# A two-layer decoder trunk on one core: residual tiles kept on chip, heads' outputs 0 to 3 stored unsplit

## The chip, the core and the metric

The kernel runs on one core of a Trainium2 chip. The metric is the device time of one execution in microseconds (us). TensorE (PE) multiplies matrices; VectorE (DVE), ScalarE (ACT) and GpSimd (POOL) work on tiles of 128 partitions; SyncE (SP) and POOL issue the DMAs between DRAM and the chip's memory. Each engine has its own queue of instructions and works it off in order; an instruction that waits for another engine or for a DMA holds up all behind it on its engine.

## The reference

One sequence of 1024 tokens, width 1024, float32, two layers, and a final normalisation.

```
h = x
n = rms_norm(h, attn_norm[0])
h = h + hybrid_mixer(n)         # layer 0: 8 heads of dilated attention, 8 of forgetting
h = h + conv_glu_ffn(rms_norm(h, ffn_norm[0]))
n = rms_norm(h, attn_norm[1])
h = h + diff_mixer(n)           # layer 1: 8 heads of differential attention
h = h + conv_glu_ffn(rms_norm(h, ffn_norm[1]))
out = rms_norm(h, final_norm)

forgetting_attention: softmax(q k^T + c_t - c_s) v, causal; c = cumsum(log_sigmoid(n w_f + b_f))
differential_attention: (softmax(q1 k1^T) - lam softmax(q2 k2^T)) v, rms_norm of each head's output
both mixers end in: concat(heads) @ w_out
conv_glu_ffn: (silu(conv3(n w_gate)) * (n w_up)) @ w_down, inner width 2816
```

## The kernel before

All tiles hold features on the 128 partitions and tokens on the free axis, so a layer's residual h is 8 feature blocks (index m) of 2 token halves (half 0 and 1) of 512 tokens: 16 tiles of 128x512. A float32 product is made of three matmuls: each operand is split into a high part (a rounded copy, made by ACT) and a low part (source minus high part, by DVE), and hi·hi, hi·lo, lo·hi are added up in PSUM. This `split` (L162) is the commonest step of the kernel.

Time runs as follows: attention of layer 0 (start to about 612 us), its feed-forward `channel(0)` (to about 1300), attention of layer 1 (about 1360 to 1862), `channel(1)` (to the end). In the attention phases `weave` (L489) merges two streams by a planned goal of work done: the *units* (one head or pair of heads and one token half: scores D, exponentials e, transposes T split into ph and pl, and the output O) and the *jobs* (projections for later heads, then the output projection, one generator step at a time). A job can carry `after`, the unit that must have ended before it starts. The compiled order of each engine's queue is fixed; the tile framework puts the instructions in it and the waits between them.

The places that matter here:

- `out_heads` (L291) takes a finished head output (o2 in layer 0, Ra in layer 1; index k from 0 to 7 in each layer). For k of 6 and 7 it is split into tiles that stay on chip (oh__, ol__). For k of 0 to 5 it is split into so_h and so_l, and both are stored to DRAM (od), 256 KB each.
- `job_load` (L429) fetches both parts again: for k of 0 to 3 behind the last projection job, so 16 loads of 256 KB in a row; for 4 and 5 later. They go through POOL's queue (`store` is a DMA on POOL, `put` one on SP).
- `job_out` (L441) is the output projection, in three jobs: heads 0 to 3 for both halves, added to the residual rt and stored to hp; heads 4 to 7 for half 0, added to the reloaded hp tile and stored again, with the sums for the norm; heads 4 to 6 for half 1 (`rest`), stored again. The last head's part of half 1 is done in `channel` (L1360), with weights o7.
- Between the second and the third job, `stats` makes the norm's rows for half 0, and `blocks` (L1174) reloads the eight hp tiles of half 0 on SP, scales each (`token_blocks`, L1118), stores it to nt, and splits it into nh and nl for the gate product. This is one generator step: all eight follow each other at once.
- `channel` (L1323) reloads the eight half-1 tiles of hp into x (tag wq, 16 slots), adds the last head's product, makes the norm, scales, and forms sums and differences with the half-0 tiles b0 (reloaded from nt: four in wq slots, four in bt slots), which are split again (`cut`, tiles bt) as operands of the feed-forward. The feed-forward's weights use the other wq slots, and POOL makes sums of weights there (L824).
- The pool `big` has 32 tiles of 128x512; nh, nl, oh__, ol__, rt and the token tiles share it.

Of the kernel before, what the change touches and what calls it, by code (L numbers as in the profile page):

```python
# [49 lines left out]
class Trunk:  # L50
# [240 lines left out]
    def out_heads(self, o, half, k):  # L291

        if k not in self.odirect:
            self.split_out(o, half, None, self.od[0][k], self.od[1][k], 0)
            return
        self.O[k, half] = (self.big.tile([P, HT], F32R, name="oh_", tag="big"),
                           self.big.tile([P, HT], F32R, name="ol_", tag="big"))
        self.split(*self.O[k, half], o)
# [37 lines left out]

    def job_rope(self, s1, s2, n, scale, dst, r):

        w1, w2 = self.wadd8(s1), self.wadd8(s2)

        def gen():
            for half in range(2):
                x1 = self.pj()
                yield from self.g_mm(x1, w1, n, half)
                ab = self.rope_a(x1, half)
                x2 = self.pj()
                yield from self.g_mm(x2, w2, n, half)
                self.rope_b(ab, x2, half, scale, dst, r)
        return Job(gen, 4 * 8 * 0.64)

    def job_plain(self, src, n, scale, dst, r):
        nc = self.nc
        w = self.wadd8(src)

        def gen():
            for half in range(2):
# [4 lines left out]
                nc.vector.tensor_tensor(o, x, n["rb"][:, c], ALU.mult)  # L361
                self.split_out(o, half, scale, dst[0], dst[1], r)
        return Job(gen, 2 * 8 * 0.64)

# [64 lines left out]
    def job_load(self, O, k, after):  # L429
# [9 lines left out]
        return Job(gen, 0.0, after)  # L439

    def job_out(self, w, ks, halves, O, base, evict, after, depth=5):  # L441

# [46 lines left out]
    def weave(self, ev, jobs, deadline, margin):  # L489
# [24 lines left out]
        st = {"job": 0, "gen": None, "done": 0.0}  # L514
        fins = set()
        lastq = max(k for k, e in enumerate(ev) if e[1] == 1)
# [607 lines left out]
    def run(self):  # L1124
# [22 lines left out]
        Os = [{}, {}]  # L1147
        self.odirect = (6, 7)
        cs = [slice(hf * HT, (hf + 1) * HT) for hf in range(2)]


        def out_jobs(l, w, base):
            st, gi, O = stF[l], 2 * l + 1, Os[l]

            def add(src, norm):
                def b(m, half):
# [17 lines left out]
            def blocks():  # L1174
                ts = []
                for m in range(10):
                    if m < 8:
                        t = f(self.big.tile([P, HT], F32R, name="t0", tag="big"))
                        self.put(t, parts[l][m][:, cs[0]])
                        ts.append(t)  # L1180
                    if m == 0:
                        rest.fetch()
                    if 0 < m < 9:
                        self.token_blocks(st, gi, 0, m - 1, ts[m - 1])
                        self.store(half0[m - 1], ts[m - 1])
                    if m > 1:
                        hl = (self.big.tile([P, HT], F32R, name=x, tag="big") for x in ("nh", "nl"))
                        st["h"][m - 2, 0], st["l"][m - 2, 0] = hl
                        self.split(st["h"][m - 2, 0], st["l"][m - 2, 0], ts[m - 2])
                yield 0.0  # L1190
# [3 lines left out]
            jobs += [self.job_out(w, [0, 1, 2, 3], [0, 1], O, *add(base, False), last(3))]  # L1194
            jobs += [self.job_load(O, k, last(k)) for k in range(4, 6)]
            jobs += [self.job_out(w, [4, 5, 6, 7], [0], O, *add(part, True), 29 if l == 0 else 13)]
            rest = self.job_out(w, [4, 5, 6], [1], O, *add(part, False), 27 if l == 0 else 14, 3)
            jobs += [Job(stats, 1.3), Job(blocks, 0.0)]
            jobs += [rest]
            return jobs  # L1200
# [14 lines left out]
        for g in range(2):  # L1215
# [3 lines left out]
            for p in range(2 * g, 2 * g + 2):  # L1219
                J0 += [self.job_plain(w[2 * p], n, -0.125, qB, p * P),  # L1220
                       self.job_plain(w[2 * p + 1], n, None, kB, p * P)]
        J0 += out_jobs(0, a["woA"], lambda m: a["xT"][m * P:(m + 1) * P, :])
# [5 lines left out]
        for g in range(4):  # L1228
            w = a["wqkC"]
            if g:  # L1230
                J1 += [self.job_v(a["wvC"][g], n, 2, P, (1, 2 * g))]
            J1 += [self.job_rope(w[4 * g], w[4 * g + 1], n, -0.125, qC, g * P),
                   self.job_rope(w[4 * g + 2], w[4 * g + 3], n, None, kC, g * P)]
        J1 += out_jobs(1, a["woC"], lambda m: hs[m])
# [88 lines left out]
        def channel(l, es, w7, F, after, mid):  # L1323
# [310 lines left out]
```

## Time and profile before

| | us |
|---|---|
| median of three runs | 2571.03 (2567.0 to 2571.26) |
| the profiled execution | 2565.89, its span 2564.1 |
| PE busy | 2467.2 (96%), 12511 matmuls |
| DVE busy | 1979.0 (77%) |
| ACT busy | 1221.5 (48%) |
| POOL busy | 721.4 (28%) |
| moved by DMA | 536.96 MB, mean 209 GB/s |

The span runs from the first to the last recorded instruction; the execution is 1.8 us longer. PE's clock has two levels, 1.2 and 2.4 GHz; a granted clock (PEclk) of 1.00 means the higher one all through a stretch. A row of waits says which engine and line waited for which other engine, line and tile. In names like oh__6277 the number tells tiles of one name apart. "<-" reads "is written from".

### The profile page before, as it was taken

What the parts mean: (1) busy time and instruction counts of PE and PEld (TensorE: products, weight loads), DVE (VectorE), ACT (ScalarE), POOL (GpSimd) and SP (SyncE); (2) the same over time, 40 slices, a digit from 0 to 9 for tenths busy, and PEclk for the clock granted to TensorE, in tenths of its full rate; (3) what the DMA queues carried; (4) which work ended last, traced back from release to release, by engine and by line L of the source; (5) the groups of instructions that cost most, each with busy time, mean ns of one, the idle gap of its engine ahead of it and who ended that gap; (6) DMA issues with size and microseconds to landing.
All of it is one profiled execution on the core that took longest, in us unless ns stands there. A gap on an engine that the chain in (4) does not pass through costs nothing.

```text
span 2564.1 us, 38450 instructions
## 1 busy us (share of the span) xinstructions
PE 2467.2 (96%) x12511; PEld 2047.6 (80%) x12511; DVE 1979.0 (77%) x3885; ACT 1221.5 (48%) x2443; POOL 721.4 (28%) x978
## 2 busy tenths in 40 slices
PE   8999999998899999999999999989888999999998
PEld 7899898776688888778888888877666888887886
DVE  7778878776988988775666888878769878977656
ACT  5456655454544344454434555545454443435433
POOL 1211112222444665100021211232225456740000
PEclk9999999998999999999999999999989999999998
DMA  5655556867766887664555555696576677766644
GB/s 192 229 172 172 178 173 216 255 204 275 216 207 219 244 241 240 205 220 167 193 202 169 197 182 193 203 288 216 179 253 198 204 238 242 248 201 231 226 130 160
DMA packets 249240, 536.96 MB, mean 209 GB/s; under 512 B 37976, under 2 KB 50896, under 8 KB 249040
## 3 DMA queue, kind: packets, MB, share of 16 engines
q1 hardware_dynamic: 179792, 320.02, 39.3%
q0 software_dynamic: 68672, 213.96, 25.1%
q8 instruction: 99, 1.62, 0.3%
q14 instruction: 101, 0.83, 0.1%
q10 hardware_dynamic: 576, 0.52, 0.1%
HBM read 362.33 MB, written 172.03 MB: 208 GB/s over the span
## 4 chain that ended last, share of the span: by engine, by line
PE 79%; DVE 8%; DMA 7%; ACT 3%; issue 2%; SPq 0%; POOL 0%; DVEq 0%; ACTq 0%; POOLq 0%
PE pj L145 67%; PE D L145 5%; PE O L145 4%; PE T L148 3%; DVE wl L131 2%; DMA wr<-in_wgate 1%; DVE bt L166 1%; PE small L145 1%; DMA wr<-in_wdown 1%; ACT wh L129 1%; DVE e L590 1%; DMA ncb<-cd 1%; ACT e L739 1%; DMA wr<-in_wqkC 1%; DMA ar<-td 1%
## 5 line engine op out<-in xcount | busy, mean ns | idle before, releaser
L145 PE MATMUL pj<-bt,wh 128*128 128x512 f32 x1760 | 554.2, 395 | 13.0 <-DVE bt L166 8.6
L145 PEld LDWEIGHTS pj<-bt,wh 128*128 128x128 f32 x1760 | 331.2, 188 | 93.5 <-DVE bt L166 11.6
L131 DVE TENSOR_TENSOR wl<-wr,wh 128x512 fp32r<-128x512 f32 (+2 forms) x340 | 235.7, 696 | 180.8 <-ACT wh L129 171.1
L145 PE MATMUL pj<-nh,wh 128*128 128x512 f32 x864 | 356.9, 413 | 16.8 <-ACT nh L232 8.6
L129 ACT ACTIVATE wh<-wr 128x512 fp32r<-128x512 f32 (+2 forms) x340 | 211.4, 624 | 290.5 <-PE pj L145 122.5
L145 PE MATMUL pj<-bt,wl 128*128 128x512 f32 x880 | 347.7, 395 | 0.0
L145 PE MATMUL pj<-nl,wh 128*128 128x512 f32 x864 | 346.2, 401 | 0.0
L145 PE MATMUL pj<-nh,wl 128*128 128x512 f32 x864 | 346.0, 401 | 0.0
L131 DVE TENSOR_TENSOR wl<-wq,wh 128x512 fp32r<-128x512 f32 x268 | 278.0, 1038 | 30.4 <-ACT wh L129 30.2
L129 ACT ACTIVATE wh<-wq 128x512 fp32r<-128x512 f32 x268 | 166.7, 628 | 239.2 <-PE pj L145 186.9
L824 POOL TENSOR_TENSOR wq<-wq 128x512 f32<-128x512 f32 x132 | 195.3, 1491 | 211.4 <-DVE wl L131 102.3
L145 PE MATMUL pj<-ah,wh 128*128 128x512 f32 (+1 forms) x628 | 248.0, 396 | 2.5 <-ACT s L1086 1.2
L145 PE MATMUL pj<-ah,wl 128*128 128x512 f32 (+1 forms) x628 | 246.2, 393 | 0.0
L145 PE MATMUL pj<-al,wh 128*128 128x512 f32 (+1 forms) x628 | 246.1, 392 | 0.0
L145 PEld LDWEIGHTS pj<-nh,wh 128*128 128x128 f32 x864 | 166.1, 192 | 49.9 <-ACT nh L232 8.6
L165 ACT ACTIVATE ph<-T 128x512 fp32r<-128x512 f32 (+3 forms) x288 | 138.9, 486 | 131.5 <-PE T L148 128.7
L145 PEld LDWEIGHTS pj<-bt,wl 128*128 128x128 f32 x880 | 165.8, 188 | 39.0
L145 PEld LDWEIGHTS pj<-nh,wl 128*128 128x128 f32 x864 | 165.5, 192 | 37.9 <-DVE wl L131 0.4
L145 PEld LDWEIGHTS pj<-nl,wh 128*128 128x128 f32 x864 | 166.2, 192 | 31.1 <-DVE nl L247 0.5
L166 DVE TENSOR_TENSOR pl<-T,ph 128x512 fp32r<-128x512 f32 (+3 forms) x288 | 157.5, 552 | 34.2 <-ACT ph L165 32.9
L148 PE MATMUL T<-ident,e 128*128 128x128 f32 x864 | 144.1, 277 | 19.2 <-DVE e L746 13.5
L145 PE MATMUL pj<-wh,nh 128*128 128x256 f32 (+1 forms) x512 | 149.0, 293 | 0.0
(476 smaller groups left out, 5339.7 us busy)
## 6 DMA issues: line engine op xcount, KB each, us to landing
wq<-in_wgate SPq DMA_DIRECT2D x88, 256.0 KB, 3.7
wq<-in_wup SPq DMA_DIRECT2D x88, 256.0 KB, 3.9
act<-v POOLq DMA_DIRECT2D x44, 512.0 KB, 3.6
td<-sc POOLq DMA_DIRECT2D x80, 256.0 KB, 4.5
wq<-in_wdown SPq DMA_DIRECT2D x80, 256.0 KB, 4.4
sd<-wq POOLq DMA_DIRECT2D x80, 256.0 KB, 4.1
ar<-td SPq DMA_DIRECT2D x80, 256.0 KB, 3.8
wr<-sd SPq DMA_DIRECT2D x80, 256.0 KB, 3.8
```

The lines of the kernel that those rows point to most:

```text
L129: nc.scalar.activation(hi[:, :n], raw[:, :n], AF.Copy)
L131: nc.vector.tensor_tensor(lo[:, :n], raw[:, :n], f(hi[:, :n]), ALU.subtract)
L145: self.last = self.nc.tensor.matmul(*args, **kw)
L148: self.last = self.nc.tensor.transpose(*args)
L165: nc.scalar.activation(hi, src, AF.Copy)
L166: nc.vector.tensor_tensor(lo, src, f(hi), ALU.subtract)
L590: self.nc.vector.tensor_tensor_reduce(out=e[:, k0:k0 + w], in0=d[:, :w], in1=in1(k0, w), scale=1.0, scalar=init, op0=ALU.add, op1=ALU.min, ...
L739: nc.scalar.activation(e[m][:, :W], e[m][:, :W], AF.Exp, scale=-1.0, bias=nm[:, m:m + 1], accum_out=ls[:, m, i4:i4 + 1])
L824: nc.gpsimd.tensor_tensor(dst, x, y, op)
```

## The change

- Heads' outputs 0 to 3 go to DRAM as they are, one store of 256 KB for each half, without a split. `fetch_raw` loads them again, one load for each half, called within the last q/k projection job of the layer when its first half is done. The new first job behind the projections, `job_split`, splits the eight loaded tiles on chip (oh__ from ol__, then ol__ in place).
- The half-0 tiles of the residual stay on chip between the second job and `blocks` (dict t0); the reload is gone. The half-1 tiles stay on chip between `rest` and `channel` (dict t1); their store to hp behind `rest` and the reload are gone. b0 takes eight wq slots.
- `blocks` yields three times behind each token tile, and each yield takes one step of `rest` if the unit that `rest` needs has ended.

```diff
     def out_heads(self, o, half, k):
+        if k in self.oraw:
+            self.store(self.od[0][k][:, half * HT:(half + 1) * HT], o)
+            return
         if k not in self.odirect:
...
     def job_plain(self, src, n, scale, dst, r, between=None):
...
                 self.split_out(o, half, scale, dst[0], dst[1], r)
+                if half == 0 and between is not None:
+                    between()
...
+    def fetch_raw(self, O, after):
+        assert after in self.fins, (after, self.fins)
+        for k in self.oraw:
+            for half in range(2):
+                O[k, half] = (self.big.tile([P, HT], F32R, name="oh_", tag="big"),
+                              self.big.tile([P, HT], F32R, name="ol_", tag="big"))
+                self.store(f(O[k, half][1]), self.od[0][k][:, half * HT:(half + 1) * HT])
+
+    def job_split(self, O):
+        def gen():
+            for k in self.oraw:
+                for half in range(2):
+                    self.split(*O[k, half], f(O[k, half][1]))
+                yield 0.0
+        return Job(gen, 0.0)
...
                 def e(m, half, ps, t):
                     nc.vector.tensor_tensor(t, t, ps, ALU.add)
-                    self.store(parts[l][m][:, cs[half]], t)
-                    if norm:
-                        self.norm_chunk(st, m, half, t, None)
+                    if half == 0 or keep is None:
+                        self.store(parts[l][m][:, cs[half]], t)
+                    if keep is not None:
+                        keep[m] = t
+                        if half == 0:
+                            self.norm_chunk(st, m, half, t, None)
...
             def blocks():
...
+                rest.fetch()
+                more = rest.gen()
+                for m in range(9):
                     if m < 8:
-                        t = f(self.big.tile([P, HT], F32R, name="t0", tag="big"))
-                        self.put(t, parts[l][m][:, cs[0]])
...
+                        self.token_blocks(st, gi, 0, m, t0[m])
+                        self.store(half0[m], t0[m])
...
+                        self.split(st["h"][m - 1, 0], st["l"][m - 1, 0], t0[m - 1])
+                    for _ in range(3):
+                        yield next(more, 0.0) if rest.after in self.fins else 0.1
+                while rest.after not in self.fins:
+                    yield 0.1
+                yield from more
...
-            jobs = [self.job_load(O, k, last(k)) for k in range(4)]
+            jobs = [self.job_split(O)]
...
-            x = [wq() for _ in range(8)]
-            for m in range(8):
-                self.put(x[m], parts[l][m][:, cs[1]])
+            x = [self.t1[l][m] for m in range(8)]
...
-            b0 = [wq() for _ in range(4)] + [f(small()) for _ in range(4)]
+            b0 = [wq() for _ in range(8)]
```

The change moves instructions at three places that the prediction speaks of.

ACT in layer 0, where the loads of heads 0 to 3 land (about 436 us in the trace before; ph is the high part of a transposed tile T, e an exponential, so_h the high part of a projection's result). Before:

```order
L165 ACTIVATE ph_6000<-T_5995 128x4x128
L165 ACTIVATE ph_6020<-T_6016 128x3x128
L165 ACTIVATE ph_6000<-T_6042 128x4x128
L681 ACTIVATE e_6032,st_6033<-e_6032,st_6033 128x256
L165 ACTIVATE ph_6020<-T_6052 128x4x128
L681 ACTIVATE e_6062,st_6063<-e_6062,st_6063 128x384
L165 ACTIVATE ph_6086<-T_6084 128x128
```

and now:

```order
L165 ACTIVATE ph_5960<-T_5955 128x4x128
L165 ACTIVATE oh__6043<-ol__6044 128x512
L165 ACTIVATE oh__6046<-ol__6047 128x512
L165 ACTIVATE oh__6049<-ol__6050 128x512
L165 ACTIVATE ph_5980<-T_5976 128x3x128
L165 ACTIVATE ph_5960<-T_6002 128x4x128
L706 ACTIVATE e_5992,st_5993<-e_5992,st_5993 128x256
L165 ACTIVATE oh__6052<-ol__6053 128x512
L165 ACTIVATE ph_5980<-T_6012 128x4x128
L165 ACTIVATE oh__6055<-ol__6056 128x512
L165 ACTIVATE oh__6058<-ol__6059 128x512
L165 ACTIVATE oh__6061<-ol__6062 128x512
```

The splits oh__ of the loaded tiles ol__ stand among the attention's copies and exponentials.

DVE in layer 0 at the token tiles (about 579 us in the trace before; t0_ and, now, rt_7191, rt_7193, rt_7195 are token tiles, gn and rb the norm's factors, nl the low part, pl the low part of a transposed tile). Before:

```order
L1120 SCALAR_TENSOR_TENSOR t0_7532<-t0_7532,gn_69,rb_7503 128x512
L1120 SCALAR_TENSOR_TENSOR t0_7540<-t0_7540,gn_69,rb_7503 128x512
L1120 SCALAR_TENSOR_TENSOR t0_7544<-t0_7544,gn_69,rb_7503 128x512
L166 TENSOR_TENSOR nl_7549<-t0_7532,nh_7548 128x512
L166 TENSOR_TENSOR pl_7476<-T_7637,ph_7475 128x4x128
L166 TENSOR_TENSOR nl_7557<-t0_7540,nh_7556 128x512
L166 TENSOR_TENSOR pl_7529<-T_7661,ph_7528 128x4x128
L166 TENSOR_TENSOR nl_7565<-t0_7544,nh_7564 128x512
L1120 SCALAR_TENSOR_TENSOR t0_7552<-t0_7552,gn_69,rb_7503 128x512
L1162 TENSOR_TENSOR rt_7536<-rt_7536,pj_7648 128x512
```

and now:

```order
L1145 SCALAR_TENSOR_TENSOR rt_7191<-rt_7191,gn_69,rb_7471 128x512
L1145 SCALAR_TENSOR_TENSOR rt_7193<-rt_7193,gn_69,rb_7471 128x512
L166 TENSOR_TENSOR pl_7444<-T_7543,ph_7443 128x4x128
L166 TENSOR_TENSOR nl_7553<-rt_7191,nh_7552 128x512
L166 TENSOR_TENSOR pl_7497<-T_7572,ph_7496 128x4x128
L1145 SCALAR_TENSOR_TENSOR rt_7195<-rt_7195,gn_69,rb_7471 128x512
L166 TENSOR_TENSOR nl_7585<-rt_7193,nh_7584 128x512
L1189 TENSOR_TENSOR rt_7502<-rt_7502,pj_7559 128x512
L131 TENSOR_TENSOR wl_7596<-wr_7592,wh_7594 128x384
L615 ISA e_7604,mn_7609<-D_7606,ncb_6837 128x512
```

The scalings of three tiles in a row and their subtractions are drawn apart; scores (ISA rows) and the next product's add stand between them.

PE at the end of layer 0's attention (about 611 us; O is the last unit's output, nh and nl times wh and wl the gate product, oh__7929 or oh__7873 times o7_ the last head's part of the output projection). Before:

```order
L145 MATMUL O_7867<-ph_7880,V_6867 128x128
L145 MATMUL O_7867<-pl_7881,V_6867 64x128
L145 MATMUL pj_7955<-nl_7573,wh_7742 128x512
L145 MATMUL pj_7955<-nh_7572,wl_7744 128x512
L145 MATMUL pj_7977<-nh_7548,wh_7803 128x512
L145 MATMUL pj_7977<-nl_7549,wh_7803 128x512
...
L145 MATMUL pj_7977<-nl_7573,wh_7803 128x512
L145 MATMUL pj_7977<-nh_7572,wl_7805 128x512
L145 MATMUL pj_8015<-oh__7929,o7_7939 128x512
L145 MATMUL pj_8015<-ol__7930,o7_7939 128x512
```

and now:

```order
L145 MATMUL O_7808<-pl_7822,V_6835 64x256
L145 MATMUL O_7808<-ph_7821,V_6835 128x128
L145 MATMUL O_7808<-pl_7822,V_6835 64x128
L145 MATMUL pj_7943<-oh__7873,o7_7883 128x512
L145 MATMUL pj_7943<-ol__7874,o7_7883 128x512
L145 MATMUL pj_7951<-oh__7873,o7_7883 128x512
L145 MATMUL pj_7951<-ol__7874,o7_7883 128x512
```

The last head's products follow directly on the last row of O; the gate products that stood between are ahead of it.

## Rows read from the trace of the kernel before

**Rows 1.** Page, busy us, share of the span, instructions of each engine
```profile
PE 2467.2 (96%) x12511; PEld 2047.6 (80%) x12511; DVE 1979.0 (77%) x3885; ACT 1221.5 (48%) x2443; POOL 721.4 (28%) x978
```

**Rows 2.** Stretches: length; busy of PE, PEld, DVE, ACT, POOL; PEclk, DMA share, GB/s
```profile
480.00:520.00 40.00, 40.00 (x226) 33.68 (x225) 27.99 (x64) 14.88 (x32) 8.63 (x16) 1.00 0.70 221
440.00:480.00 40.00, 35.68 (x193) 28.99 (x192) 29.03 (x78) 20.17 (x46) 13.41 (x25) 0.91 0.89 286
560.00:600.00 40.00, 34.38 (x157) 27.43 (x156) 32.24 (x69) 17.75 (x35) 11.33 (x21) 0.83 0.63 213
600.00:640.00 40.00, 35.17 (x163) 27.84 (x162) 22.76 (x43) 17.65 (x32) 8.63 (x16) 0.91 0.78 282
680.00:720.00 40.00, 34.74 (x139) 26.69 (x138) 36.37 (x43) 18.50 (x32) 23.43 (x23) 0.91 0.65 196
1680.00:1720.00 40.00, 33.84 (x171) 28.06 (x170) 29.14 (x69) 18.10 (x42) 13.14 (x25) 0.91 0.95 293
1800.00:1840.00 40.00, 30.15 (x155) 24.52 (x156) 33.89 (x89) 22.29 (x52) 7.02 (x13) 0.87 0.43 156
1840.00:1880.00 40.00, 31.54 (x144) 24.27 (x143) 19.75 (x40) 13.10 (x31) 7.01 (x13) 0.96 0.55 181
1880.00:1920.00 40.00, 34.83 (x134) 27.42 (x135) 29.68 (x51) 20.89 (x36) 12.18 (x19) 0.87 0.83 298
1920.00:1960.00 40.00, 35.28 (x141) 27.51 (x140) 39.75 (x45) 19.79 (x37) 22.79 (x20) 0.91 0.66 202
```

**Rows 3.** Chain that ended last, 425 to 460: start, us, what
```profile
434.25 17.20 DMA ncb<-cd
```

**Rows 4.** DMA issues 425 to 470: count, KB each, us to landing; one in time order
```profile
oh__6277<-od POOLq DMA_DIRECT2D x1, 256.0 KB, 4.7
...
ol__6282<-od POOLq DMA_DIRECT2D x1, 256.0 KB, 8.7
...
oh__6301<-od POOLq DMA_DIRECT2D x1, 256.0 KB, 12.8
...
432.08 0.54 POOL L197 DMA_DIRECT2D ol__6282<-od  x1
```

**Rows 5.** ACT in order of time, 428 to 446: start, us, instruction, idle before
```profile
438.33 0.49 ACT L165 ACTIVATE ph<-T 128x384 fp32r<-128x384 f32 x1 [1.37 <-PE T L148]
```

**Rows 6.** Waits of SP's queue, 540 to 575: us in total, times, longest
```profile
SPq L194 <- DMA hp<-rt: 7.7, 3, 3.4
```

**Rows 7.** DVE and POOL in order of time, three places
```profile
579.21 2.08 DVE L1120 SCALAR_TENSOR_TENSOR t<-t,gn,rb 128x512 f32<-128x512 f32 x3 [1.51 <-ACT rb L282]
...
676.95 5.33 DVE L166 TENSOR_TENSOR bt<-wq,bt 128x512 fp32r<-128x512 f32 x1
...
677.58 4.14 POOL L824 TENSOR_TENSOR wq<-wq 128x512 f32<-128x512 f32 x3
```

**Rows 8.** Waits of PE, 540 to 700
```profile
PE pj L145 <- DVE bt L166: 5.3, 4, 3.8
...
PE D L145 <- DVE mn L590: 2.1, 1, 2.1
PE pj L145 <- DVE wq L1364: 2.0, 2, 1.5
```

**Rows 9.** PE in order of time, 610 to 632
```profile
611.59 0.22 PE L145 MATMUL O<-pl,V 128*64 128x128 f32 x1
...
614.96 0.39 PE L145 MATMUL pj<-oh__7929,o 128*128 128x512 f32 x1
```

**Rows 10.** Waits of DVE, 1670 to 1700
```profile
DVE Ra L795 <- DMA rt<-sr: 6.4, 1, 6.4
```

**Rows 11.** Waits of PE, 1795 to 1990
```profile
PE T L148 <- DVE e L746: 4.5, 1, 4.5
```

**Rows 12.** Tile Ra, 1440 to 1470: durations in ns, first and last start
```profile
L795 DVE SCALAR_TENSOR_TENSOR Ra<-Ra,subg,rt x1: 748/748/748, 1448.1 to 1448.1; 128x512 f32<-128x512 f32 x1
...
L759 ACT ACTIVATE Ra<-O x1: 597/597/597, 1461.6 to 1461.6; 128x512 f32<-128x512 f32 x1
```

More of the change, by code (lines that the diff above doesn't have):

```diff
@@ L335, in pj, with job_rope @@
         return self.psp.tile([P, HT], F32, name="pj", tag=tag)
-    def job_rope(self, s1, s2, n, scale, dst, r):
+    def job_rope(self, s1, s2, n, scale, dst, r, between=None):
         w1, w2 = self.wadd8(s1), self.wadd8(s2)
@@ L348, in gen, with job_plain @@
                 self.rope_b(ab, x2, half, scale, dst, r)
+                if half == 0 and between is not None:
+                    between()
         return Job(gen, 4 * 8 * 0.64)
-    def job_plain(self, src, n, scale, dst, r):
+    def job_plain(self, src, n, scale, dst, r, between=None):
         nc = self.nc
@@ L362, in gen @@
                 self.split_out(o, half, scale, dst[0], dst[1], r)
+                if half == 0 and between is not None:
+                    between()
         return Job(gen, 2 * 8 * 0.64)
@@ L514, in weave @@
         st = {"job": 0, "gen": None, "done": 0.0}
-        fins = set()
+        fins = self.fins = set()
         lastq = max(k for k, e in enumerate(ev) if e[1] == 1)
@@ L1147, in run, with add @@
         Os = [{}, {}]
-        self.odirect = (6, 7)
+        self.odirect, self.oraw = (6, 7), (0, 1, 2, 3)
         cs = [slice(hf * HT, (hf + 1) * HT) for hf in range(2)]
+        self.t1 = {}
         def out_jobs(l, w, base):
             st, gi, O = stF[l], 2 * l + 1, Os[l]
-            def add(src, norm):
+            def add(src, keep=None):
                 def b(m, half):
@@ L1174, in blocks @@
             def blocks():
-                ts = []
-                for m in range(10):
+                rest.fetch()
+                more = rest.gen()
+                for m in range(9):
                     if m < 8:
-                        t = f(self.big.tile([P, HT], F32R, name="t0", tag="big"))
-                        self.put(t, parts[l][m][:, cs[0]])
[L1180 to L1186, printed above, removed]
-                        hl = (self.big.tile([P, HT], F32R, name=x, tag="big") for x in ("nh", "nl"))
-                        st["h"][m - 2, 0], st["l"][m - 2, 0] = hl
-                        self.split(st["h"][m - 2, 0], st["l"][m - 2, 0], ts[m - 2])
@@ L1190, in blocks @@
-                yield 0.0
+                        self.token_blocks(st, gi, 0, m, t0[m])
+                        self.store(half0[m], t0[m])
+                    if m > 0:
+                        hl = (self.big.tile([P, HT], F32R, name=x, tag="big") for x in ("nh", "nl"))
+                        st["h"][m - 1, 0], st["l"][m - 1, 0] = hl
+                        self.split(st["h"][m - 1, 0], st["l"][m - 1, 0], t0[m - 1])
+                    for _ in range(3):
+                        yield next(more, 0.0) if rest.after in self.fins else 0.1
@@ L1191, in out_jobs @@
+                while rest.after not in self.fins:
+                    yield 0.1
+                yield from more
+            t0, self.t1[l] = {}, {}
             last = lambda k: 4 * k + 3 if l == 0 else 2 * k + 1
             part = lambda m: parts[l][m]
-            jobs = [self.job_load(O, k, last(k)) for k in range(4)]
-            jobs += [self.job_out(w, [0, 1, 2, 3], [0, 1], O, *add(base, False), last(3))]
+            jobs = [self.job_split(O)]
+            jobs += [self.job_out(w, [0, 1, 2, 3], [0, 1], O, *add(base), last(3))]
@@ L1195, in out_jobs @@
             jobs += [self.job_load(O, k, last(k)) for k in range(4, 6)]
[L1196 to L1199, printed above, removed]
+            jobs += [self.job_out(w, [4, 5, 6, 7], [0], O, *add(part, t0), 29 if l == 0 else 13)]
+            rest = self.job_out(w, [4, 5, 6], [1], O, *add(part, self.t1[l]), 27 if l == 0 else 14, 3)
@@ L1200, in out_jobs @@
+            jobs += [Job(stats, 1.3), Job(blocks, rest.cost)]
             return jobs
@@ L1220, in run @@
                 J0 += [self.job_plain(w[2 * p], n, -0.125, qB, p * P),
-                       self.job_plain(w[2 * p + 1], n, None, kB, p * P)]
+                       self.job_plain(w[2 * p + 1], n, None, kB, p * P,
+                                      (lambda: self.fetch_raw(Os[0], 15)) if p == 3 else None)]
         J0 += out_jobs(0, a["woA"], lambda m: a["xT"][m * P:(m + 1) * P, :])
@@ L1232, in run @@
             J1 += [self.job_rope(w[4 * g], w[4 * g + 1], n, -0.125, qC, g * P),
-                   self.job_rope(w[4 * g + 2], w[4 * g + 3], n, None, kC, g * P)]
+                   self.job_rope(w[4 * g + 2], w[4 * g + 3], n, None, kC, g * P,
+                                 (lambda: self.fetch_raw(Os[1], 7)) if g == 3 else None)]
         J1 += out_jobs(1, a["woC"], lambda m: hs[m])
```

## The prediction

> **What bounds the kernel now.** I read the page's busy line first: TensorE (PE) is busy 96% of the span, VectorE (DVE) 77% [rows 1]. There is no other engine to hide behind; what a change can give is the time in which PE stands or runs at its lower clock. So the next view was a table of 40 us stretches. A quiet stretch (480 to 520) has PE busy for all 40 us at clock 1.00. For the others I take as lost (40 minus PE busy) plus (1 minus clock) times 40. In layer 0 this gives 7.9 us for 440 to 480, 12.4 for 560, 8.4 for 600, 8.9 for 680: 37.6. In layer 1 it is 9.8 for 1680, 15.1 for 1800, 10.1 for 1840, 10.4 for 1880, 8.3 for 1920: 53.7 [rows 2]. The reader is to see that each large loss pairs a stand of some us with a clock of 0.83 to 0.96; at 0.91 that is a further 3.6 us in 40, the lower of the two levels (1.2 against 2.4 GHz) for about 7 us. Then I asked in each stretch who PE waited for, and what that one waited for.
>
> The nine stretches lie where the change works: the fetch of the heads' outputs (440, 1680), the token tiles (560, 1800), the end of attention (600, 1840) and the cuts of the second half (680, 1880 to 1960).
>
> **The change part by part.** Per layer it takes out 8 stores and 8 loads of heads' outputs, 8 loads of first-half residual tiles, and 8 stores and 8 loads of second-half ones: 40 transfers of 256 KB, 80 in all. Matmuls, splits and adds keep their number; only their place moves. So the whole effect is in waits.
>
> *Fetch, layer 0 (lost 7.9).* PE's stand here ends a chain in which one transfer, the forgetting bias ncb, took 17.20 us [rows 3]; it was queued among the 16 loads, which land 4.7 us after issue at first and 12.8 at the end [rows 4]. With 8 loads ncb should come at least the 4 us earlier that matter. Against that: the splits now stand on ScalarE (ACT) among the attention's own copies, in its fixed order, and ACT waits where a load is late. The fourth raw load is the sixth transfer of POOL's queue in this burst; the one in that place before (ol__6282, issued at 432.08) took 8.7 us [rows 4], so it lands at 440.8. Behind its split (some 0.65 us, by the 0.49 of a copy of 384 columns [rows 5]) stands the copy of T that ran at 438.33 [rows 5]: it now starts at 441.4, 3.1 us late, with three more splits before the next copies. Bounds: minus 8 (loads land as early as the first, 4.7) to plus 4 (ACT's stand reaches PE, and the clock falls again). I take minus 2, since both happen.
>
> *Token tiles, layer 0 (lost 12.4).* SP loses its 8 reloads, each of which waited for a store to land (7.7 us in all [rows 6]) with the weight loads queued behind it. On DVE eight scalings and eight subtractions ran nearly back to back from 579, three scalings alone taking 2.08 us [rows 7], and PE's scores waited 2.1 us for DVE [rows 8]. Now they come one tile at a time, between matmuls. Bounds minus 12 to 0 (the work on DVE is the same, and may be late elsewhere); I take minus 6. A new wait: the scaling is done in place on the tile whose store to DRAM must have landed, and behind it on DVE stand the low halves of transposed probabilities. The scaling of before stood behind the same landing and a reload on top, so I price this at nothing.
>
> *End of attention, layer 0 (lost 8.4).* The eight adds of the last head's contribution no longer wait for reloaded tiles; PE waited 2.0 us for them [rows 8]. But PE's order now has the last head's matmuls straight behind the last O matmul. Before, 14 others stood between: O's last began at 611.59, the first of the last head at 614.96 [rows 9], and PE was busy throughout. The chain behind O (copy, add, split) takes that long whatever the order, so PE now stands about 3 us there. Of the 8.4 lost, some 4 go by the adds; minus 1, bounds minus 6 to plus 5.
>
> *Cuts, layer 0 (lost 8.9).* PE waited 5.3 us for bt [rows 8], the split token sums, while DVE was busy for 36 of 40 us [rows 2]. The adds that head this chain waited for reloads and start some us sooner. One subtraction in the chain took 5.33 us while three sums ran on POOL; three scalings of the same size took 2.08 together, 0.69 each [rows 7]. Bounds minus 9 to plus 6; I take minus 6.
>
> The rule that speaks against this: the Trainium skill, "SBUF — State Buffer", section "Who interferes with whom", says that a DVE instruction with two SBUF inputs contends with a GpSimd instruction that reads SBUF and that whoever starts first blocks the other for its whole length. The 5.33 us row agrees with it. The sums would then be a price of the change, as in the second rival.
>
> *Layer 1.* The same four places. Fetch (lost 9.8): DVE waited 6.4 us for rt<-sr, a small round trip through DRAM that sat in the burst of 16 loads [rows 10]; with 8 it returns sooner. ACT has six raw splits in a row here. Minus 6, bounds minus 10 to plus 4. Token tiles (15.1): PE waited 4.5 us on one late DVE result [rows 11]; minus 7, bounds minus 13 to 0. End (10.1 and half of the next stretch, 15 together): the wait for the adds goes, those for the last head's normalisation stay; minus 5, bounds minus 9 to plus 4. Cuts (13): minus 6, bounds minus 11 to plus 6.
>
> *What I price at nothing.* The raw store now reads the head's own tile (o2, Ra), so the next head's write to it waits for the landing. In layer 1 such a tile was finished at 1448.1 and written anew at 1461.6 [rows 12], 13.5 us later, and the longest landing of a transfer of this size in a burst was 12.8 [rows 4]. If that cover were gone, ACT or DVE would stand some 2 us at each of 16 places, and the time would be up by 20 or more.
>
> **Sum.** Layer 0: 2 + 6 + 1 + 6 = 15. Layer 1: 6 + 7 + 5 + 6 = 24. Together minus 39 us. DVE is busy for 29 to 40 of 40 us in seven of the nine stretches [rows 2], so a stand that is taken out partly comes back behind the same engine; I count three quarters, minus 29. The profiled execution lasted 2565.9 us, 1.8 more than its span; less 29 that is 2537. The median of the runs, 2571.0, lies 5.1 above that execution, and I forecast it: 2571 − 29 = 2542 us.
>
> **Rivals.**
> - *Waits change place.* ACT's stand at the raw splits and PE's 3 us at the last head take back most of what the transfers gave; half of the gain at token tiles (13) and cuts (12) stays. For it: both orders above are fixed. Against: those stands are short. Fetches and ends 0, the rest minus 12: 2559.
> - *POOL's sums meet the cuts.* Four of the sixteen wq slots were free for weights while the second half was made; now eight are, so two more sums per layer can start before and within the cuts. Each held DVE for about 1.5 us (5.33 less 0.69, over three [rows 7]). Then cuts give plus 3 per layer and a fallen clock of 3.6 instead of minus 6: 39 becomes 39 − 12 − 13 = 14: 2557. Against: the sums were in the cuts already, and DVE starts sooner.
> - *Nothing to gain.* The transfers were hidden, and the losses are those of the dependencies themselves (last head, norms): 2571. Against: 17.20 us for ncb and 6.4 for rt<-sr are waits for transfers.
> - *ACT stands behind the raw loads: slower.* At the two fetches all of the attention's exponentials are queued behind splits of loads. If the fourth load lands after about 444 (as late as the last of before, 12.8 us from issue), T's copies are 6 us late, PE runs out of projection matmuls, stands 6 to 8 us twice per fetch and has its clock lowered (3.6 each). That is about 20 us per layer, 40 in all, against 29 gained: 2582. For it: the loads still come in one burst. Against: half the bytes are in it.
> - *All of it comes.* The losses of both layers go to a third, minus 60: 2511.
>
> **How the numbers follow.** Forecast 0.46 (its own range 2527 to 2553); waits change place 0.13; POOL's sums 0.09; nothing 0.07; slower 0.14; all of it 0.11. What a measurement can tell from no change is 0.2%, 5 us. Faster: 0.46 + 0.11 + 0.09 + 0.11 of the 0.13 = 0.77. Within 5 us: 0.07 + 0.02 = 0.09. Slower: 0.14. The range 2513 to 2573 leaves out the better half of the last case and nearly all of the slower one.
>
> **What would show it.** Right: in 440 to 480 and 1680 to 1720 PE near 38 of 40 and clock 1.00, ncb landing in under 13 us; no wait of PE for the adds; no DVE run of more than three token-tile instructions; bt waits under 2 us. Steps wrong: PE waiting for ph or T right behind a split of oh__; a stand above 4 us at the last head; DVE instructions of 2 us or more in the cuts. The forecast is wrong as a whole if the clock still falls in seven or more of the nine stretches, or if o2 or Ra is waited for by a store's landing.

## The result, and the profile after

The changed kernel takes 2525.4 us (median of 4 runs) against 2571.2 for the kernel before, a ratio of 0.9824 with a 95% interval of 0.9802 to 0.9846: 45.8 us less, where 29 were forecast (2542; range 2513 to 2573). Measured once more in another job it took 2533.1, a ratio of 0.9861 (0.9839 to 0.9882). The two ratios are 0.4% apart, each with an interval of some 0.2% to either side, so the gain is best read as 36 to 46 us.

The page's busy line of the changed kernel, as in [rows 1]; its profiled execution lasted 2523.6 us:

```profile
PE 2445.1 (97%) x12511; PEld 2034.3 (81%) x12511; DVE 1976.4 (78%) x3885; ACT 1219.2 (48%) x2443; POOL 702.6 (28%) x930
```

DVE and ACT are as busy as before, to within 3 us, so nothing was saved there. The stretches of the changed kernel, with the columns of [rows 2] (the program runs some 20 us ahead from 640 us on, and some 40 at the end; so the fetch of layer 1, in 1680 to 1720 before, lies in 1640 to 1680 here):

```profile
440.00:480.00 40.00, 38.63 (x219) 31.35 (x220) 36.24 (x96) 24.57 (x55) 14.46 (x27) 1.00 0.85 262
560.00:600.00 40.00, 37.19 (x215) 30.78 (x214) 35.39 (x76) 20.41 (x41) 7.58 (x14) 1.00 0.46 152
600.00:640.00 40.00, 34.91 (x148) 27.32 (x148) 29.73 (x53) 19.73 (x37) 14.32 (x22) 0.96 0.88 309
640.00:680.00 40.00, 34.27 (x139) 26.93 (x140) 39.86 (x47) 22.35 (x41) 26.65 (x21) 0.96 0.61 189
680.00:720.00 40.00, 40.00 (x175) 32.46 (x174) 33.72 (x51) 16.93 (x27) 18.23 (x19) 1.00 0.61 186
1640.00:1680.00 40.00, 36.24 (x189) 29.87 (x189) 33.55 (x90) 24.14 (x68) 15.32 (x29) 0.96 0.89 299
1680.00:1720.00 40.00, 39.71 (x220) 32.89 (x218) 30.91 (x92) 20.02 (x56) 5.95 (x11) 1.00 0.64 214
1800.00:1840.00 40.00, 35.75 (x176) 28.95 (x176) 29.41 (x68) 18.99 (x48) 5.93 (x11) 0.91 0.49 163
1840.00:1880.00 40.00, 32.84 (x137) 25.98 (x136) 33.90 (x50) 20.23 (x38) 14.87 (x20) 0.91 0.79 264
1880.00:1920.00 40.00, 37.04 (x157) 28.88 (x156) 39.56 (x51) 22.30 (x42) 21.64 (x19) 1.00 0.61 197
1920.00:1960.00 40.00, 40.00 (x174) 32.41 (x173) 31.18 (x48) 15.86 (x26) 18.56 (x19) 1.00 0.65 197
```

The reader is to see the clock: 1.00 in six of the eleven rows, where before it was below 1.00 in all nine stretches. In the whole trace PE's stands (times of 0.15 us and more in which it runs nothing) went from 88.8 to 68.2 us, and the time at the lower clock, without that at the very end, from 71.7 to 23.8 us, at half speed a gain of 24 us. The second profile of the same kernel has nearly the same stands, 69.4 us, but 44.4 us at the lower clock, a gain of 14. The mean granted clock of the spans says the same: 0.983 before, 0.992 and 0.988 now. So between a third and somewhat more than half of the gain is clock that came back, and the two profiles of one kernel, 6.5 us apart, differ in the clock and hardly in the stands.

To say where the time came from I compared the start of the same matmul in two traces (those that write O, or read bt or ah, counted from the program's start). The lead over the kernel before grows in these steps:

| us gained in the profile, from the same matmul | fetch, layer 0 (430 to 486) | tokens to cuts, layer 0 (486 to 713) | rest of channel 0 and next start (713 to 1394) | fetch, layer 1 (1665 to 1718) | tokens to cuts, layer 1 (1718 to 1972) |
|---|---|---|---|---|---|
| forecast, whole terms | 2 | 13 | 0 | 6 | 18 |
| changed kernel | 4.9 | 14.3 | -0.1 | 3.5 | 21.0 |
| changed kernel, again | 5.2 | 13.3 | -1.0 | 2.8 | 16.8 |
| E1 fetch as before | 0.3 | 8.8 | -2.3 | 1.0 | 12.7 |
| E2 half 1 reloaded | 4.8 | 1.2 | -2.4 | 3.5 | 11.1 |
| E3 burst | 4.5 | 6.2 | -3.9 | 5.5 | 9.2 |
| E4 half 0 reloaded | 4.8 | 8.3 | -0.5 | 6.5 | 11.0 |
| E5 fetch called late (same order) | 4.7 | 10.7 | -4.2 | 2.8 | 21.2 |
| E11 copies added | -2.4 | 10.6 | -2.4 | 2.2 | 17.8 |
| E12 two parts undone | -0.3 | 0.9 | -5.0 | -0.1 | 10.1 |

The middle column is a stretch in which the change does nothing; with its -0.1 to -5.0 (and -8.6 in E8's first profile) it shows that a step of one profile can be read to some 5 us and no finer. Only up to 640 us do profiles of the same code agree within 1 us.

### The profile page after: what moved, and what is told of

It is laid out like the page before. It is cut to its first block, busy times and chain, and to the rows that moved or that the text cites. A ratio compares the mean times of both kernels' runs of the same rounds, so it can differ in the third digit from the quotient of the medians.

```text
span 2521.9 us, 38243 instructions
## 1 busy us (share of the span) xinstructions
PE 2445.1 (97%) x12511; PEld 2034.3 (81%) x12511; DVE 1976.4 (78%) x3885; ACT 1219.2 (48%) x2443; POOL 702.6 (28%) x930
## 4 chain that ended last, share of the span: by engine, by line
PE 80%; DMA 6%; DVE 6%; issue 4%; ACT 2%; POOL 1%; SPq 0%; ACTq 0%; DVEq 0%; POOLq 0%
PE pj L145 66%; PE D L145 5%; PE O L145 4%; PE T L148 4%; DVE wl L131 1%; PE small L145 1%; DMA wr<-in_wgate 1%; DMA wr<-in_wdown 1%; DMA ar<-act 1%; ACT wh L129 1%; DMA rt<-sr 1%; DMA ar<-td 1%; DVE e L615 1%; DVE bt L166 1%; DVE e L771 0%
## 5 line engine op out<-in xcount | busy, mean ns | idle before, releaser
L145 PE MATMUL pj<-nh,wh 128*128 128x512 f32 x864 | 354.6, 410 | 17.8 <-ACT nh L232 8.8
L849 POOL TENSOR_TENSOR wq<-wq 128x512 f32<-128x512 f32 x132 | 202.4, 1538 | 213.9 <-DVE wl L131 106.8
```

The source lines that it names most:

```text
L145: self.last = self.nc.tensor.matmul(*args, **kw)
L849: nc.gpsimd.tensor_tensor(dst, x, y, op)
```

## The experiments

All are built from the changed kernel. Times are medians; the ratio is to the kernel before, timed in the same job, and "costs" is the ratio less 0.9842 (the mean of the changed kernel's two), times 2569 us. The three timings of the changed kernel's order of instructions (E5 is the third, as shown there) gave 0.9824, 0.9861 and 0.9842, so every cost may be off by some 5 us, all of one job in the same direction, and a cost under 6 us tells nothing.

| | us | ratio (95%) | costs, us |
|---|---|---|---|
| E1 fetch as before | 2545.1 | 0.9906 (0.9891 to 0.9921) | 16 |
| E2 half 1 reloaded, slots as before | 2550.3 | 0.9929 (0.9912 to 0.9945) | 22 |
| E3 burst | 2542.5 | 0.9893 (0.9872 to 0.9913) | 13 |
| E4 half 0 reloaded | 2540.7 | 0.9889 (0.9874 to 0.9904) | 12 |
| E5 fetch called late | 2531.8 | 0.9842 (0.9825 to 0.9860) | 0 |
| E6 slots as before | 2532.8 | 0.9853 (0.9838 to 0.9868) | 3 |
| E7 layer 1 drawn apart | 2547.2 | 0.9905 (0.9890 to 0.9920) | 16 |
| E8 two steps, and again | 2534.4, 2531.5 | 0.9864, 0.9857 | 6, 4 |
| E11 copies added | 2541.4 | 0.9893 (0.9872 to 0.9914) | 13 |
| E12 E1 and E2 together | 2560.8 | 0.9963 (0.9949 to 0.9977) | 31 |

**E1**, the fetch as before.

```diff
-        self.odirect, self.oraw = (6, 7), (0, 1, 2, 3)
+        self.odirect, self.oraw = (6, 7), ()
-            jobs = [self.job_split(O)]
+            jobs = [self.job_load(O, k, last(k)) for k in range(4)]
```

> The changed kernel with the heads' outputs 0 to 3 treated as before (split first, both parts stored, 16 loads behind the last projection); residual tiles and token tiles stay as changed. By the theory that each place brings its own part (lead of the changed kernel's profile: 4.9 us at the fetch of layer 0, 3.5 at that of layer 1), it takes 8.4 us more than the changed kernel, about 2534, all of it at 440 to 460 and at 1670 to 1690, with the clock falling again at both. By the rival that the fetch's gain is only moved (ACT's stand at the raw splits is given back later), it stays within 3 us of the changed kernel, 2525 to 2528.

It cost about 16 us. The stand at 452 came back whole. E1's chain of waits (start, us, what):

```profile
434.18 17.18 DMA ncb<-cd
```

and the PE waits from 425 to 500 (sum in us, count, longest) of E1, then of the kernel before:

```profile
PE T L148 <- DVE e L709: 4.2, 1, 4.2
...
PE T L148 <- DVE e L684: 4.2, 1, 4.2
```

The 17.18 is the 17.20 of [rows 3]. The size expected was too small: by the table E1 also loses 2 to 6 us in the rest of layer 0 and 4 to 9 in that of layer 1, where its code is that of the changed kernel (which has three rows there: its two profiles and E5). E1 changes two things at once, the number of loads and the place of the splits, and no run here parts them.

**E11**, the changed kernel with traffic added that nothing waits for.

```diff
                 self.store(f(O[k, half][1]), self.od[0][k][:, half * HT:(half + 1) * HT])
+                self.store(self.dr.tile([P, HT], F32, name=f"cp{after}_{k}_{half}"),
+                           self.od[0][k][:, half * HT:(half + 1) * HT])
```

> The changed kernel with a copy from DRAM to DRAM of 256 KB behind each of the eight raw loads of a layer, which nothing on the chip waits for: as many transfers in the burst as before, but no more waits. If traffic and POOL's queue are what the fetch gained by, PE stands again at 440 to 460 (3 us or more, ncb late) and it takes 5 to 20 us more, 2530 to 2545. If it was the order of the splits and the waits, it stays within 3 us.

It cost 13 us (8 against the changed kernel timed in the same job), but it is not the run that was meant. The tile framework put each copy on POOL's queue right behind the store that it reads, not behind the raw load. The copies of E11 in layer 0:

```profile
L197 POOL DMA_DIRECT2D cp<-od x8: 540/552/778, 130.4 to 329.1; - x8
```

and those of layer 1 run from 1416.3 to 1619.2: none is in the burst of 425 to 470. What E11's trace does show there is another thing. The last three of the eight raw loads are issued from 435.42 on, 1.3 us later than the last three of the changed kernel, and land 11.3 to 13.2 us after issue (6.9 to 7.5 in the changed kernel). ACT stands behind each, in its fixed order. ACT in E11, in order of time, and PE's waits from 425 to 500:

```profile
446.77 0.63 ACT L165 ACTIVATE oh__6065<-ol__6066 128x512 fp32r<-128x512 f32 x1 [3.33 <-DMA ol__6066<-od]
...
450.02 0.63 ACT L165 ACTIVATE oh__6075<-ol__6076 128x512 fp32r<-128x512 f32 x1 [1.28 <-DMA ol__6076<-od]
...
PE T L148 <- DVE e L711: 5.0, 1, 5.0
PE T L148 <- DVE pl L166: 2.0, 1, 2.0
```

The e that PE waits for 5.0 us is one that ACT makes behind these splits; for ncb nothing waits. So E11 says nothing on the number of transfers. It shows the fourth rival of the prediction (ACT behind the raw loads) at work: with landings some 4 us later it takes back the whole gain of this fetch, and the place of the splits does count. Why the three loads came late is not shown.

**E5**, the eight raw loads called behind the last projection instead of within it.

```diff
+            self.fetch_raw(O, after)     # at the start of job_split
...
-                                      (lambda: self.fetch_raw(Os[0], 15)) if p == 3 else None)]
+                                      None)]
```

> The changed kernel, but its eight raw loads per layer are called behind the last projection job (where the 16 were), not in its middle. If it is the number of loads that pays, it stays within 4 us of the changed kernel, 2525 to 2529. If it is the earlier call, it is at the level of the kernel with the fetch undone, 2540 to 2545, with PE standing 3 us or more at 440 to 460 and at 1670 to 1690.

No cost, but nothing was moved either: name by name, every engine's queue in E5's trace has the order of the changed kernel. The first raw load on POOL, in E5 and then in the changed kernel, waits for the same matmul to free its tile (E5's program runs 0.8 us ahead here):

```profile
427.56 0.54 POOL L197 DMA_DIRECT2D ol__6238<-od  x1 [7.67 <-PE pj L145]
...
428.42 0.54 POOL L197 DMA_DIRECT2D ol__6041<-od  x1 [7.67 <-PE pj L145]
```

So E5 doesn't tell an early call from a late one. It is a third timing of the changed kernel's order.

**E2**, half 1 stored and reloaded, b0 in four wq and four bt slots, and **E6**, the slots alone.

```diff
# E2 alone
-            rest = self.job_out(w, [4, 5, 6], [1], O, *add(part, self.t1[l]), 27 if l == 0 else 14, 3)
+            rest = self.job_out(w, [4, 5, 6], [1], O, *add(part), 27 if l == 0 else 14, 3)
...
-            x = [self.t1[l][m] for m in range(8)]
+            x = [wq() for _ in range(8)]
+            for m in range(8):
+                self.put(x[m], parts[l][m][:, cs[1]])
...
# E2 and E6
-            b0 = [wq() for _ in range(8)]
+            b0 = [wq() for _ in range(4)] + [f(small()) for _ in range(4)]
```

> The changed kernel with the second half's residual tiles stored and loaded again as before, and with the half-0 token sums in four wq and four bt slots as before; fetch and token tiles as changed. By the theory of places it loses what the end of attention and the cuts gained beyond the token tiles: 4 to 6 us per layer, 8 to 12 in all, about 2535, with PE waiting for the adds of the last head (2 us or more). By the rival that spreading the token tiles gave all of the later gain, it stays within 3 us of the changed kernel.

> The changed kernel with only the half-0 token sums put back into four wq and four bt slots, so that the four wq slots freed serve the weights all the more: it tells what the use of slots is worth apart from the reload. By the rival on POOL's sums (those that run in the cuts hold DVE 1.5 us each), the more slots are free the earlier sums run and the more they cost: some 3 to 6 us slower than the changed kernel. By the theory that waits for tiles were what counted, no change: within 3 us, 2522 to 2528.

E2 cost 22 us, E6 3, which is within the scatter: some 19 us hang on the store, the reload and the eight wq slots that the reloaded tiles take (E2 leaves four wq slots free, as before; the changed kernel eight, E6 twelve). The waits show where; PE in E2 from 595 to 700, then DVE:

```profile
PE small L145 <- DVE dg L273: 5.4, 2, 4.1
PE pj L145 <- DVE bt L166: 4.8, 2, 4.0
...
PE pj L145 <- DVE wq L1395: 0.8, 1, 0.8
...
DVE wq L1395 <- DMA wq<-hp: 3.1, 1, 3.1
```

DVE stands 3.1 us for a reloaded tile, but the adds themselves (L1395) cost PE 0.8 us. What is late behind them is the norm's spread (dg, 5.4; none and 1.2 in the changed kernel's two profiles) and then bt. That is the chain add, norm, scale, cut: a delay at its head shows at its later members.

E6 also bears on the rival on POOL's sums. With eight slots free they did start earlier (the first at 620.9 us in the changed kernel, at 645.6 before); with twelve, six had started by 650 us instead of four or five, and no cost can be measured.

**E3**, all eight token tiles in one step, and **E4**, half 0 reloaded but drawn apart.

```diff
# E3
-                    for _ in range(3):
-                        yield next(more, 0.0) if rest.after in self.fins else 0.1
...
+                yield 0.0
...
-            jobs += [Job(stats, 1.3), Job(blocks, rest.cost)]
+            jobs += [Job(stats, 1.3), Job(blocks, 0.0), rest]
# E4
+                ts = []
+                for m in range(8):
+                    t = f(self.big.tile([P, HT], F32R, name="t0", tag="big"))
+                    self.put(t, parts[l][m][:, cs[0]])
+                    ts.append(t)
...
```

> The changed kernel with its token tiles made in one step again, all eight behind each other, and the third output job behind them; the tiles stay on chip. By the theory of places the spread is worth the larger part of the token tiles' gain, 5 us in layer 0 and 6 in layer 1: about 2536, with PE waiting for scores behind DVE again (2 us or more per layer). By the rival that the reloads were what cost there, it stays within 3 us of the changed kernel.

> The changed kernel with the first half's residual tiles loaded again before the token tiles are made (eight loads on SP), which are still made one at a time between matmuls. By the theory that the spread carries this place it takes 1 to 3 us more than the changed kernel, 2526 to 2528; by the rival that the reloads (SP waiting for stores, the weights behind them) carry it, 10 us more, about 2535.

Both cost 12 to 13 us. E3's PE waits from 560 to 625, then E4's from 540 to 600:

```profile
PE T L148 <- DVE pl L166: 4.9, 1, 4.9
...
PE small L145 <- DVE o L250: 1.9, 1, 1.9
PE pj L145 <- DVE rt L1189: 0.4, 1, 0.4
```

In E3 the transposes wait 4.9 us behind DVE's burst. In E4 no such wait is left; its stand is one of 1.9 us at the norm (0.3 in the changed kernel), and the clock is 0.91 in its stretch of 560 to 600 (1.00 in the changed kernel). Each of my two theories took one of the two as the whole; both parts carry the place.

**E12**, E1 and E2 together.

> The changed kernel with two parts undone at once: the fetch of the heads' outputs, and the second half's residual tiles with the slots of b0; what stays is the first half's tiles and the drawn-out token tiles. Undone alone they cost 20 and 25 us. If the shares add up, this takes 45 us more than the changed kernel, 2570, no faster than the kernel before. If the parts share their gain (a stand and a lowered clock that either of them brings back), it stays clearly under the sum: 2550 to 2560.

31 us, where the two alone sum to 38; all four parts sum to 63, and the change gives 36 to 46. The scatter between jobs bears on these sums: against the first timing of the changed kernel it is 36 where the two sum to 48, and 82 for the four where the change gives 45; against the second 26 and 29, and 44 for 36. So the four sum to more than the whole on either, which fits parts that share their gain, but how much they share is not shown, and of E1 and E2 not whether.

**E7**, layer 1's token tiles drawn apart.

```diff
-                        yield next(more, 0.0) if rest.after in self.fins else 0.1
+                        yield next(more, 0.0) if rest.after in self.fins else (0.1 if l == 0 else 1.2)
-            jobs += [Job(stats, 1.3), Job(blocks, rest.cost)]
+            jobs += [Job(stats, 1.3), Job(blocks, rest.cost + (0.0 if l == 0 else 27 * 1.2))]
```

> The changed kernel with another count of work for layer 1's token tiles: a step that finds the third output job not ready yet counts as 1.2 instead of 0.1, so that the planner draws the eight tiles apart there too. In the changed kernel's profile the sixteen DVE instructions of layer 1 still follow each other from 1793 to 1803 and PE stands 7.1 us. By the theory that the burst is the cause the stand shrinks to under 3 us and the clock stays up: 2517 to 2521. By the rival that PE would wait at the end of attention anyway (it has no products left until the third job may start), the stand comes back later: within 3 us of the changed kernel.

It is 16 us slower. The stand of 7.1 us is gone, but the added count makes the planner run the output projection earlier, and PE now waits for its operands. E7's PE waits from 1740 to 1830:

```profile
PE pj L145 <- ACT oh__19835 L165: 3.9, 1, 3.9
...
PE pj L145 <- ACT oh__19979 L165: 1.5, 1, 1.5
```

It tells that this way of drawing apart doesn't pay, not that none would. No version here beats the changed kernel.

**E8**, two steps of the third job behind each tile instead of three (`range(2)`), and the changed kernel again.

> The changed kernel with two steps of the third output job behind each token tile instead of three; a control. The four undone parts cost 15 to 25 us each, more together than the change gave. If each place holds its own share, this small shift costs 0 to 4 us, 2525 to 2529, and leaves layer 1 as it is. If the time hangs on the exact order of the queues (any shift costs), it is 8 us or more slower, 2533 or above.

> The kernel with two steps per token tile once more, on the same chip as the changed kernel. If its 9 us are a property of its order, it is again 6 us or more slower than the changed kernel and loses some 6 us again in the down projection of layer 0, which the edit does not touch. If they were scatter, the two are within 4 us.

> The changed kernel once more, unaltered, as a measure of scatter: its time should be 2521 to 2531 and its profile's lead over the kernel before, place by place, within 2 us of the first profile. If the stretch between the two attentions (1060 to 1390 of before), where the change does nothing, differs by 4 us or more between the two profiles, single profiles can't be read finer than that.

In the first job E8 looked 9 us slower than the changed kernel (2534.4 against 2525.4); side by side in one job they are equal (2531.5 and 2533.1). The 9 us were scatter between jobs, and the 8.6 us that E8's first profile lost from 713 to 1394 were 3.8 the second time. The changed kernel's own second profile kept within 2 us up to the cuts of layer 1, where it lost 4.

## Why the prediction was right, and where its sizes were off

The way and, in the main, the mechanism held: nothing was computed faster, waits went and the clock came back. The terms as summed, 39 us, are what the two profiles gained, 42.8 and 36.9 us at the last ah matmuls. **The step that was mis-sized is the discount to three quarters.** I argued that a stand taken out comes back behind the same busy DVE. In sum it did not: DVE stays at 29 to 40 of 40 us in the rows above, and yet the gain is that of the undiscounted terms; at the cuts alone did most of the wait stay. Had I not discounted, the forecast would have been 2532. But that the sum comes out is partly luck: of its terms two were too small (fetch and token tiles of layer 0) and two too large (cuts of layer 0, fetch of layer 1). Term by term:

*Fetch, layer 0: 2 forecast, 5 measured.* Both halves are in ACT's rows of the changed kernel in order of time:

```profile
439.25 0.63 ACT L165 ACTIVATE oh__6049<-ol__6050 128x512 fp32r<-128x512 f32 x1 [1.51 <-DMA ol__6050<-od]
439.78 0.96 ACT L165 ACTIVATE ph<-T 128x384 fp32r<-128x384 f32 x2
```

ACT does stand for the fourth raw load, and the copy of T behind it is late: 439.78 against 438.33 in [rows 5]. It is 1.5 us, not 3.1, because that load took 7.4 us, not 8.7 [rows 4], and the last of the burst 7.5 (count, KB, us to landing):

```profile
ol__6050<-od POOLq DMA_DIRECT2D x1, 256.0 KB, 7.4
...
ol__6062<-od POOLq DMA_DIRECT2D x1, 256.0 KB, 7.5
```

I had taken the landing from the same place in a queue of 16. PE waits 1.2 us there (for pl of T), and no row shows DVE waiting for ncb. Matmul by matmul the lead over the kernel before falls by 2.2 us up to 449, where the splits stand, and rises by 7.1 from 455 to 470, where before PE had stood and run at the lower clock. The slower rival would have needed that load after 444; E11, where the last three loads land at 446.8 to 449.9, shows what such landings cost.

*Tokens to cuts, layer 0: 13 forecast, 13 to 14 measured* (11 in E5), but distributed otherwise. PE's waits of the changed kernel from 530 to 690, against [rows 8]:

```profile
PE pj L145 <- ACT sc L956: 6.4, 4, 2.4
PE pj L145 <- ACT o L165: 2.6, 1, 2.6
PE pj L145 <- ACT bt L165: 2.2, 1, 2.2
PE pj L145 <- DVE bt L166: 2.1, 1, 2.1
PE pj L145 <- DVE rt L1189: 0.4, 1, 0.4
PE small L145 <- DVE o L250: 0.3, 1, 0.3
```

At the token tiles nothing is left but 0.7 us and the clock is full, so that place gave nearly all of its 12.4 and not 6: by matmuls 11.0 us from 540 to 605 in both profiles. The stand behind the last O is there as forecast (2.6 us, "about 3"), and the end (605 to 672) gave 1 and 0 us where 1 was forecast (-4 in E5's profile). The cuts (672 to 713) gave 2 and not 6: PE still waits 4.3 us for bt, 5.3 before.

*Fetch, layer 1: 6 forecast, 3 measured.* The wait for rt<-sr became shorter and is not gone. The changed kernel from 1640 to 1705, DVE's wait, the transfer in the chain that ended last, and PE's wait:

```profile
DVE Ra L820 <- DMA rt<-sr: 4.0, 1, 4.0
...
1657.94 8.67 DMA rt<-sr
...
PE pj L145 <- DVE rt L328: 3.0, 1, 3.0
```

The product L328, which PE waits for at 1669.6, stands on DVE right behind this wait (4.1 and 3.2 us in the second profile). The round trip, from the issue of sr<-ctd to DVE's start behind rt<-sr, took 10.3 us where it had taken 12.9; its second transfer alone, with half the loads about it, took 8.7 and before 6.9. So "with 8 it returns sooner" held for 2.4 us of the 6.4.

*Tokens to cuts, layer 1: 18 forecast, 17 to 21 measured, with one step wrong.* I wrote that the tiles come one at a time. In layer 1 they do not. DVE in the changed kernel:

```profile
1793.10 2.08 DVE L1145 SCALAR_TENSOR_TENSOR rt<-rt,gn,rb 128x512 f32<-128x512 f32 x3
1795.09 0.69 DVE L166 TENSOR_TENSOR nl<-rt,nh 128x512 fp32r<-128x512 f32 x1
...
1802.02 0.69 DVE L166 TENSOR_TENSOR pl<-T,ph 128x512 fp32r<-128x512 f32 x1
```

and PE at the same place:

```profile
1795.23 0.40 PE L145 MATMUL pj<-oh__19878,wl 128*128 128x512 f32 x1
1802.76 0.48 PE L148 MATMUL small<-ident,Ra 128*128 128x128 f32 x1 [7.13 <-DVE pl L166]
```

Here the third job may start only after unit 14 of 16, later than the planner reaches the tiles, so each of the 27 yields finds it not ready and counts 0.1, and all go by at once. PE stands 7.1 us, longer than any stand of before (6.2) but that at the very start. DVE's order in layer 1 would have shown it ahead; I had used that of layer 0 alone. By matmuls, tokens and end together (1718 to 1861) gave 14 us where 12 were forecast, and the cuts 7 in the first profile and 3 in the second, where 6 were. That the place gained all the same is the chain behind the stand: PE's waits from 1717 to 1960 are

```profile
PE small L148 <- DVE pl L166: 7.3, 2, 7.1
...
PE pj L145 <- DVE bt L166: 2.3, 3, 1.2
PE pj L145 <- DVE rt L1393: 2.1, 2, 1.3
```

while of the waits of before, from 1795 to 1990, that for T (4.5 us, [rows 11]) and these two, for the norm's spread and for nt, are gone:

```profile
PE small L145 <- DVE dg L273: 3.2, 2, 1.6
...
PE pj L145 <- DMA wq<-nt: 1.5, 1, 1.5
```

The wait for the adds did not go in layer 1 as it did in layer 0: 2.1 us (rt L1393), 2.4 before. E2 and E4 take 6 to 10 us of this place away again.

*Priced at nothing:* no row shows a wait for the landing of a store from o2 or Ra.

*POOL's sums:* the sign named for them, DVE instructions of 2 us or more in the cuts, is there. DVE and POOL of the changed kernel in order of time:

```profile
664.19 4.37 DVE L166 TENSOR_TENSOR bt<-rt,bt 128x512 fp32r<-128x512 f32 x1
...
663.91 4.09 POOL L849 TENSOR_TENSOR wq<-wq 128x512 f32<-128x512 f32 x3
```

The rule of the Trainium skill that VectorE and GpSimd contend for SBUF ("SBUF — State Buffer", section "Who interferes with whom") agrees with this row and with the 5.33 us of [rows 7]; that the one that starts first blocks the other, [rows 7] do not show, since the subtraction starts at 676.95, ahead of the three sums at 677.58. This contention may be why the cuts gave less than forecast. No run tells: none takes the sums away, and more of them early cost nothing that could be measured (E6).

Open: why undoing the fetch (E1) also costs time from tokens to cuts in both layers, where the code is the same. In layer 0 E1's steps are those of the changed kernel up to 640 us. From there to 713 PE's waits are longer (16.6 us from 595 to 705, against 13.3 and 11.7 in the changed kernel's two profiles), but E5, in the order of the changed kernel, loses 3 us there too, so part of it may be scatter.

## What to carry to other kernels

When an engine is 96% busy, list its stands and low-clock stretches first and price a change by those it touches. Add up the terms as the rows give them; don't discount for a suspected shift unless a row shows the next wait. When an edit draws work apart by a planner's count, look at the order in every place where the code runs: the same lines gave a spread in one layer and a burst in the other. Undo the parts one by one, but expect that they may sum to more than the whole (63 against 40 us here), and time the kernel itself again in another job before reading differences under 10 us. Before reading an experiment's time, find its edit in its trace: a framework that orders the queues moved E11's copies some 100 us away from where the source has them, and E5's call moved nothing at all.

## What the runs showed of the hardware

- The landing time of one transfer is not told by the number of loads alone. ncb (512 KB) took 17.2 us among 16 loads of 256 KB, before and in E1, and held nobody among 8. But with 8 loads in either kernel, the last three took 6.9 to 7.5 us in the changed one and 11.3 to 13.2 in E11, where they were issued 1.3 us later; and rt<-sr took 8.7 us among 8 loads, 6.9 among 16.
- The lower clock did not follow each stand in these traces, and not the same stand each time: the changed kernel stands 2.6 us up to 600.1 with the clock at 1.00 in its first profile, and in its second, up to 599.0, the clock is at the lower level for 3.4 us from 600.3 on. In the kernel before, stands of 2.1 and 1.1 us that end at 590 and 592 went with 6.8 us at half speed from 591.3 on. Over the whole trace nearly the same stands (68.2 and 69.4 us) came with 23.8 and 44.4 us of it.
